# A linear recurrence in chunks: one state update for two heads, values and state in tiles of their own, and a binding on the output weights' preparation

## The chip, the cores and the metric

The kernel runs on one core of one Trainium2 chip. Its metric is the device time of one execution in microseconds (us). Three runs of the kernel before took 1298.18, 1294.85 and 1297.59 us, median 1297.59. The profile is of one further execution, which took 1294.26 us.

The engines are TensorE (PE in the profile; PEld is its loading of weights), VectorE (DVE), ScalarE (ACT) and GpSimd (POOL); SyncE (SP) issues most transfers, in the order of one queue.

## The reference, cut to what matters

One layer mixes 2048 tokens of width 1024 in three ways, gates the results and projects them. The change touches the first two ways, which are one recurrence with different sizes (GLA: 4 heads, keys of 64, values of 128; HGRN: 4 heads, keys and values of 64):

```python
CHUNK = 64
h = rms_norm(x) * (1.0 + scale[:, None, :]) + shift[:, None, :]
p = h @ w_in[l]                                  # 1024 -> 3600 columns
...
def chunk_gated_linear_attn(q, k, v, g):
    ...
    def step(state, inp):
        q_c, k_c, v_c, g_c = inp
        b_cum = jnp.cumsum(g_c, axis=2)
        decay = jnp.exp(jnp.where(causal, diff, -jnp.inf))
        scores = jnp.einsum('bhtd,bhsd,bhtsd->bhts', q_c, k_c, decay)
        o_c = (jnp.einsum('bhts,bhsv->bhtv', scores, v_c)
               + jnp.einsum('bhtd,bhdv->bhtv', q_c * jnp.exp(b_cum), state))
        b_last = b_cum[:, :, -1:, :]
        state = (jnp.exp(b_last[:, :, 0, :, None]) * state
                 + jnp.einsum('bhsd,bhsv->bhdv', k_c * jnp.exp(b_last - b_cum), v_c))
        return state, o_c
...
o_a = merge_heads(rms_norm(o_a) * gla_norm_w[l]) * jax.nn.silu(ga)
y = jnp.concatenate([o_a, o_b, o_c], axis=-1) @ w_out[l]
x = x + gate[:, None, :] * y
```

So an output of a chunk is scores times values plus decayed queries times the state, and the state goes from chunk to chunk.

## The kernel before

The work runs in stages. Projections come first: queries and keys to about 205 us, values and attention columns to about 385 us. The forget stage (to about 449 us) makes the running sums of the decays (`decay_sums`, L527 to L537): a scan gives bc; picked columns SM and their exponentials SE hold three numbers per chunk and channel. SE's middle third is the decay over a whole chunk; L533 copies it into SX, crossing it to the other 64 partitions. Then the stick-breaking attention runs to about 870 us, the recurrence from 870 to 1058 us, and the output projection to the end.

**The recurrence** (`gla_fast`, `gla_tail`) takes 16 groups, here numbered 0 to 15, of 512 tokens in 8 chunks of 64. Four groups make a pair of heads; groups 0 to 7 are GLA, 8 to 15 HGRN. The two heads of a pair lie on partitions 0 to 63 and 64 to 127. Per group:

- SP loads bc (decay sums), qt (queries), kt (keys), Vn (values, tokens on partitions) and W (L824, L825).
- ACT, DVE and POOL make eP (scaled queries, L901 or L906), eN (scaled keys, written into bc or kt) and kd (keys for the state); DVE writes M's half of decayed queries (L909).
- PE forms the scores scp (L917). ACT copies them to S, and POOL writes their causal part into M's other half.
- PE transposes kd (ptk, L836), ACT copies it to KTt, and PE multiplies it by Vn to U (L847), the increments of the state.
- DVE makes the states one chunk after another (L858): one instruction per chunk and head, on 64 partitions each.
- PE multiplies W by M (L870): one matmul of contraction depth 128 per chunk and head, scores and values on one half of the rows, queries and state on the other. The state of head h stands on the half opposite to the head, so that head's values fit on its own half.

The tiles U are single-buffered: the U of a group waits for the state updates of the group before. W has two buffers, so the load of W for a group waits for o of the group two before.

**Order.** PE's order here is written out by hand (`manual_schedule`): scp and ptk of a group, three gate steps (nine matmuls of L260), U, nine more, o of the group before, and then the next group. These gate steps are projections that fill PE; their weights come over SP into tiles tagged `wraw` and are split on ACT (whi) and DVE (wlo). On DVE, ACT, POOL and SP the order comes from a scheduler that places instructions by its own model of time.

**Output weights.** `scale_wo(0)` is started at group 8 and goes one step in each of groups 8 to 11. A step loads 512 KB of w_out into wr (L1019), which has the same tag `wraw` and so the same two buffers as the gate weights; POOL multiplies it by the gate row; DVE makes wh (L1023) and wl (L1024). The tag's turn in this stretch is: gate weights of j = 4, wr of steps 0 and 1, gate weights of j = 5, wr of steps 2 and 3, gate weights of j = 6 and 7. The gates' steps reach j = 5 at the end of the first nine matmuls of group 10, j = 6 at the start of group 13 and j = 7 in group 15. A buffer is free for its next load when DVE has made the wlo or wl of its last contents.

Of the kernel before, what the change touches and what calls it, by code (L numbers as in the profile page):

```python
# [42 lines left out]
def hybrid_mixer_kernel(ctx, tc, x, c, w_ada, b_ada, w_in, w2, bg, gnw, lbl, hnw,  # L43
# [764 lines left out]
    def load_values(pools, pr, g, GT, Wn):  # L808
# [8 lines left out]
        def new_w():  # L817
            return [pools.tile([P, NB, dv], F32, tag=f"W{h}", name=f"W{h}", bufs=2) for h in range(2)]
        W = Wn if Wn is not None else new_w()
        if Wn is None:  # L820
            nc.gpsimd.memset(W[0][64:128, 0, :], 0.0)
            nc.gpsimd.memset(W[1][0:64, 0, :], 0.0)
        vr = vcols.rearrange("(n p) d -> p n d", p=CB)
        nc.sync.dma_start(W[0][0:64], vr[:, :, 0:dv])  # L824
        nc.sync.dma_start(W[1][64:128], vr[:, :, dv:2 * dv])  # L825
        return Vn, W, new_w() if g + 1 < T // GT else None

    def gla_tail(gr_, pp, pr, g, GT, M, kd, dec, Vn, W, Wn):
# [48 lines left out]
    def gla_fast(pairs, gp, gr_, pp, scp):  # L877

        for pr in pairs:
# [3 lines left out]
            Wn = None  # L883
            for g in range(T // GTF):
# [42 lines left out]
                yield gla_tail(gr_, pp, pr, g, GTF, M, kd, SX[:, pr, g, :], Vn, W, Wn)

    def gla_exact(gp, pp):
# [5 lines left out]
        M = gp.tile([P, 2, GT + NB], F32, name="M")  # L935
        nc.gpsimd.memset(M, 0.0)
        for pr in (2, 3, 0, 1):
# [3 lines left out]
            Wn = None  # L941
            for g in range(T // GT):
# [25 lines left out]
                def level(Xk, Xq, mi):  # L968
# [6 lines left out]
                    for h in range(2):  # L975
                        hs = slice(h * 64, (h + 1) * 64)
                        nc.vector.copy_predicated(
                            v3(M[hs, h, 0:GT]), mx[hs, mi:mi + 1, :].broadcast_to((64, NB, CB)), sc[hs])
# [23 lines left out]
                for h in range(2):  # L1002
                    nc.vector.tensor_copy(M[(1 - h) * 64:(2 - h) * 64, h, :], Qs[h * 64:(h + 1) * 64, :])
                dec = gp.tile([P, NB], F32, tag="dec", name="dec")
                for h in range(2):
                    orow = slice((1 - h) * 64, (2 - h) * 64)
                    nc.vector.tensor_copy(dec[orow], M[orow, h, GT:GT + NB])
                for _ in gla_tail(gp, pp, pr, g, GT, M, kt, dec, Vn, W, Wn):
# [309 lines left out]
```

## Time and profile before

| | us |
|---|---|
| median of three runs | 1297.59 |
| the profiled execution | 1294.26 |
| its span on the core | 1292.2 |
| PE busy | 1212.9 (94%) |
| PEld busy | 991.8 (77%) |
| DVE busy | 742.1 (57%) |
| ACT busy | 471.7 (37%) |
| POOL busy | 162.9 (13%) |

The profiled execution has 2.1 us around its span. The busy shares are means over stages with different limits: a stage is read by its own windows, its chain of waits, and the timeline of the engine that waits. In the rows below a line such as "L870" is one of the kernel before; a releaser behind "<-" is what ended the idle time before the instruction.

### The profile page before, as it was taken

How to read it: one execution, taken by the hardware profiler on the slowest of the kernel's cores; microseconds unless marked ns; L12 is line 12 of the kernel's file. 1: busy time of each engine (PE TensorE's matmuls, PEld its weight loads, DVE VectorE, ACT ScalarE, POOL GpSimd, SP SyncE). 2: the span in 40 equal slices, each digit the busy share in tenths (PEclk: the TensorE clock that was granted, in tenths of full speed). 3: DMA queues.
4: the chain of work that ended last, by engine and by line, in shares of the span. 5: the costliest groups of instructions: out<-in, count | busy, mean ns of one | idle time of the engine just before them, and what ended most of it. 6: DMA issues, size and time to landing. Idle time of an engine off the chain costs nothing.

```text
span 1292.2 us, 22081 instructions
## 1 busy us (share of the span) xinstructions
PE 1212.9 (94%) x8682; PEld 991.8 (77%) x8682; DVE 742.1 (57%) x1268; ACT 471.7 (37%) x860; POOL 162.9 (13%) x197
## 2 busy tenths in 40 slices
PE   7899999999999789999999999998978897999997
PEld 7777789899998667777777776766867774777775
DVE  4866325700009873535545488877776768765652
ACT  3376423421115342322333244543333434253621
POOL 3210000000003300000000001012432312010000
PEclk8999999999999989999999999998988997999999
DMA  9765442422133341322323323127877657464621
GB/s 265 240 232 180 147 126 91 143 82 86 46 99 112 126 106 54 92 72 86 100 68 86 109 73 92 34 62 238 264 222 208 195 174 241 133 224 132 203 82 51
DMA packets 177566, 173.73 MB, mean 134 GB/s; under 512 B 39625, under 2 KB 131882, under 8 KB 177454
## 3 DMA queue, kind: packets, MB, share of 16 engines
q1 hardware_dynamic: 144970, 128.70, 33.7%
q10 hardware_dynamic: 32484, 43.54, 9.7%
q8 instruction: 70, 1.15, 0.4%
q14 instruction: 42, 0.34, 0.1%
HBM read 113.47 MB, written 58.73 MB: 133 GB/s over the span
## 4 chain that ended last, share of the span: by engine, by line
PE 62%; DVE 13%; DMA 6%; issue 5%; ACT 2%; POOL 1%; SPq 0%; ACTq 0%; POOLq 0%; DVEq 0%
PE av L750 6%; PE acc L154 5%; PE acc L156 5%; PE acc L155 5%; PE acc L166 4%; PE acc L168 4%; PE acc L167 4%; PE pt L738 4%; PE acc L260 4%; PE y L1194 4%; PE y L1192 4%; PE y L1193 4%; DMA kt<-s_kb 2%; DVE W L858 2%; DVE f L734 2%
## 5 line engine op out<-in xcount | busy, mean ns | idle before, releaser
L734 DVE TENSOR_TENSOR_SCAN f<-f 128x512 f32<-128x512 f32 (+3 forms) x160 | 169.9, 1091 | 22.0 <-ACT f L728 11.9
L154 PE MATMUL acc<-hTh,whi 128*128 128x512 f32 x400 | 160.1, 402 | 9.9 <-ACT st L185 4.3
L156 PE MATMUL acc<-hTh,wlo 128*128 128x512 f32 x400 | 157.5, 394 | 0.0
L155 PE MATMUL acc<-hTl,whi 128*128 128x512 f32 x400 | 157.4, 394 | 0.0
L166 PE MATMUL acc<-whi,hTh 128*128 128x256 f32 (+1 forms) x512 | 146.2, 285 | 1.5 <-ACT stt L193 1.5
L168 PE MATMUL acc<-whi,hTl 128*128 128x256 f32 (+1 forms) x512 | 145.8, 285 | 0.0
L167 PE MATMUL acc<-wlo,hTh 128*128 128x256 f32 (+1 forms) x512 | 145.6, 284 | 0.0
L260 PE MATMUL acc<-hTh,whi 128*128 128x512 f32 x240 | 103.8, 432 | 1.7 <-ACT hTh L244 1.7
L260 PE MATMUL acc<-hTl,whi 128*128 128x512 f32 x240 | 97.9, 408 | 4.3 <-DVE hTl L250 4.3
L1192 PE MATMUL y<-wh,hTh 128*128 128x512 f32 x256 | 101.8, 398 | 0.0
L1193 PE MATMUL y<-wl,hTh 128*128 128x512 f32 x256 | 101.6, 397 | 0.0
L728 ACT ACTIVATE f<-zt 128x512 f32<-128x512 f32 (+3 forms) x160 | 82.1, 537 | 52.9 <-DVE f L734 24.7
L1194 PE MATMUL y<-wh,hTl 128*128 128x512 f32 x256 | 100.1, 395 | 0.4 <-DVE hTl L1160 0.4
L166 PEld LDWEIGHTS acc<-whi,hTh 128*128 128x128 f32 x512 | 97.8, 191 | 1.9 <-ACT stt L193 1.7
L154 PEld LDWEIGHTS acc<-hTh,whi 128*128 128x128 f32 x400 | 75.5, 189 | 29.9 <-ACT st L185 5.6
L167 PEld LDWEIGHTS acc<-wlo,hTh 128*128 128x128 f32 x512 | 97.8, 191 | 0.1
L168 PEld LDWEIGHTS acc<-whi,hTl 128*128 128x128 f32 x512 | 97.8, 191 | 0.1
L260 PE MATMUL acc<-hTh,wlo 128*128 128x512 f32 x240 | 97.4, 406 | 0.0
L750 PE MATMUL av<-PT,V 128*64 128x128 f32 x960 | 89.7, 282 | 0.6 <-DVE PT L743 0.6
L156 PEld LDWEIGHTS acc<-hTh,wlo 128*128 128x128 f32 x400 | 75.3, 188 | 17.0 <-issue 1.4
L738 PE MATMUL pt<-ident,f 128*128 128x128 f32 x544 | 87.0, 283 | 0.9 <-DVE f L734 0.7
L155 PEld LDWEIGHTS acc<-hTl,whi 128*128 128x128 f32 x400 | 75.6, 189 | 15.2 <-issue 1.0
(206 smaller groups left out, 2106.8 us busy)
## 6 DMA issues: line engine op xcount, KB each, us to landing
wraw<-in_w_in_dram SPq DMA_DIRECT2D x36, 512.0 KB, 4.9
xt<-in_x_dram SPq DMA_DIRECT2D x16, 512.0 KB, 5.2
wa<-in_w_ada_dram SPq DMA_DIRECT2D x16, 512.0 KB, 5.6
Q<-s_qc SPq DMA_DIRECT2D x64, 128.0 KB, 3.1
ot<-s_o SPq DMA_DIRECT2D x32, 256.0 KB, 3.4
gt<-s_gate SPq DMA_DIRECT2D x32, 256.0 KB, 4.2
r<-in_x_dram SPq DMA_DIRECT2D x16, 512.0 KB, 5.6
out_dram<-r SPq DMA_DIRECT2D x15, 512.0 KB, 2.7
```

The costliest lines, as they stand in the source:

```text
L154: mm(ps, hi[:, k, :], th[:, k, :], start=(k == 0), stop=False)
L155: mm(ps, hi[:, k, :], tl[:, k, :], start=False, stop=False)
L156: mm(ps, lo[:, k, :], th[:, k, :], start=False, stop=(k == KT - 1))
L166: mm(o, th[:, k, s], hi[:, k, 0:ncols], start=(k == 0), stop=False)
L167: mm(o, th[:, k, s], lo[:, k, 0:ncols], start=False, stop=False)
L168: mm(o, tl[:, k, s], hi[:, k, 0:ncols], start=False, stop=(k == KT - 1))
L260: mm(ps, a[:, k, :], b[:, k, :], start=(k == 0 and i == 0), stop=(k == KT - 1 and i == 2))
L734: nc.vector.tensor_tensor_scan(fr, fr, fr, carry[u], op0=ALU.mult, op1=ALU.bypass)
L750: last[0] = mm(av[u * 64:(u + 1) * 64, :], (Dd if diag else V)[J][:, b, :], PT[:, b, :], start=diag, stop=(J == 0 and b == 0))
L1192: mm(y, oh[:, k, us], wh, start=(k == 0), stop=False)
L1193: mm(y, oh[:, k, us], wl, start=False, stop=False)
L1194: mm(y, ol[:, k, us], wh, start=False, stop=(k == KT - 1))
```

## The change

SX and its 32 copies are gone. W is parted into Vv (values, each head on its own half) and St (states of both heads in one tile, each on its own half). The U of a head goes to its own half, so one DVE instruction of 128 partitions updates both heads' states: 124 instead of 248 of L858. M is parted into Ms (causal scores) and Qd (decayed queries); Qd takes one instruction of 128 partitions instead of two of 64. Each matmul of o becomes two of contraction depth 64 that add up: Ms with Vv, then Qd with St. That is 32 a group instead of 16; as a float32 matmul is two passes here (L870 has 256 rows in eight groups), 64 passes instead of 32. The step of `scale_wo(0)` in groups 8 to 11 is issued under `issue_after` with the group's last state update. This binds instructions on that update's engine, DVE: wh and wl of a step stand behind the updates of its group. Loads and POOL's product are not bound. The memset of the first state is one instead of two; `rp0` and `open_h` change places. The same edits are made in the branch for strong decays (`gla_exact`), of which the trace has no row.

The core of the diff:

```diff
-        for h in range(2):
-            nc.vector.tensor_copy(SX[(1 - h) * 64:(2 - h) * 64, pr, n, :],
-                                  SE[h * 64:(h + 1) * 64, pr, n, NBF:2 * NBF])
...
-        def new_w():
-            return [pools.tile([P, NB, dv], F32, tag=f"W{h}", name=f"W{h}", bufs=2) for h in range(2)]
-        W = Wn if Wn is not None else new_w()
-        if Wn is None:
...
+
+        def new_s():
+            return pools.tile([P, NB, dv], F32, tag="St", name="St", bufs=2)
+        St = Sn
+        if St is None:
+            St = new_s()
+            nc.gpsimd.memset(St[:, 0, :], 0.0)
+        Vv = pools.tile([P, NB, dv], F32, tag="Vv", name="Vv", bufs=2)
         vr = vcols.rearrange("(n p) d -> p n d", p=CB)
-        nc.sync.dma_start(W[0][0:64], vr[:, :, 0:dv])
-        nc.sync.dma_start(W[1][64:128], vr[:, :, dv:2 * dv])
-        return Vn, W, new_w() if g + 1 < T // GT else None
-
-    def gla_tail(gr_, pp, pr, g, GT, M, kd, dec, Vn, W, Wn):
+        for h in range(2):
+            nc.sync.dma_start(Vv[h * 64:(h + 1) * 64], vr[:, :, h * dv:(h + 1) * dv])
+        return Vn, Vv, St, new_s() if g + 1 < T // GT else None
...
             for h in range(2):
-                orow = slice((1 - h) * 64, (1 - h) * 64 + 64)
-                mm(U[n % 2][orow, n // 2, :], KTt[rs, n // 2, h * 64:(h + 1) * 64],
+                mm(U[n % 2][h * 64:(h + 1) * 64, n // 2, :], KTt[rs, n // 2, h * 64:(h + 1) * 64],
                    Vn[rs, n // 2, h * dv:(h + 1) * dv], start=True, stop=True)
         for n in range(NB):
-            for h in range(2):
-                orow = slice((1 - h) * 64, (1 - h) * 64 + 64)
-                if n + 1 < NB:
-                    dst = W[h][orow, n + 1, :]
...
-                nc.vector.scalar_tensor_tensor(dst, W[h][orow, n, :], dec[orow, n:n + 1],
-                                               U[n % 2][orow, n // 2, :],
-                                               op0=ALU.mult, op1=ALU.add)
+            if n + 1 < NB:
+                dst = St[:, n + 1, :]
+            elif Sn is not None:
+                dst = Sn[:, 0, :]
+            else:
+                continue
+            om[0] = nc.vector.scalar_tensor_tensor(dst, St[:, n, :], dec[:, n:n + 1], U[n % 2][:, n // 2, :],
+                                           op0=ALU.mult, op1=ALU.add)
         yield
 
...
-        o = pp.tile([P, no, GT], F32, tag="o", name="o")
+        o = pp.tile([P, no, 512], F32, tag="o", name="o")[:, :, 0:GT]
         for n in range(NB):
             ns = slice(n * CB, (n + 1) * CB)
-            for h in range(2):
-                dst = o[:, h, ns] if gla else o[h * 64:(h + 1) * 64, 0, ns]
-                mm(dst, W[h][:, n, :], M[:, h, ns], start=True, stop=True)
+            for x, y, first in ((Vv, Ms, True), (St, Qd, False)):
+                for h in range(2):
+                    hs = slice(h * 64, (h + 1) * 64)
+                    dst = o[:, h, ns] if gla else o[hs, 0, ns]
+                    mm(dst, x[hs, n, :], y[hs, ns], start=first, stop=not first)
```
```diff
-                M = gr_.tile([P, 2, GTF], F32, tag="M", name="M", bufs=3)
+                Ms, Qd = (gr_.tile([P, GTF], F32, tag=t, name=t, bufs=3) for t in ("Ms", "Qd"))
...
-                for h in range(2):
-                    nc.vector.tensor_tensor(v3(M[(1 - h) * 64:(2 - h) * 64, h, :]),
-                                            v3(eP[h * 64:(h + 1) * 64]),
-                                            per_chunk(0)[h * 64:(h + 1) * 64], op=ALU.mult)
+                nc.vector.tensor_tensor(v3(Qd), v3(eP), per_chunk(0), op=ALU.mult)
...
-                    nc.gpsimd.affine_select(v3(M[hs, h, :]), v3(S[hs]),
+                    nc.gpsimd.affine_select(v3(Ms[hs]), v3(S[hs]),
                                             pattern=[[0, NBF], [1, CB]], base=0,
                                             channel_multiplier=-1, compare_op=ALU.is_ge, fill=0.0)
-                yield gla_tail(gr_, pp, pr, g, GTF, M, kd, SX[:, pr, g, :], Vn, W, Wn)
+                yield gla_tail(gr_, pp, pr, g, GTF, Ms, Qd, kd, SE[:, pr, g, NBF:2 * NBF],
+                               Vn, Vv, St, Sn)
...
                     ws = scale_wo(0, pw0, gr_.tile([P, 512], F32, name="gb", bufs=1))
-                next(ws, None)
+                if i >= 8:
+                    with tc.issue_after(om[0].ins):
+                        next(ws, None)
```

The scheduler's order changes with it. On DVE, in group 5, the order before mixes updates of both heads with other work; W_8966 and W_8967 are the two heads' tiles, U_9178 and U_9179 even and odd chunks, wh_9948 and wl_9949 output weights, eP and bc of group 7.

```order
L858 SCALAR_TENSOR_TENSOR W_8966<-W_8966,SX,U_9178 64x128
L901 SCALAR_TENSOR_TENSOR eP<-qt,eP 128x512
L858 SCALAR_TENSOR_TENSOR W_8967<-W_8967,SX,U_9178 64x128
L1023 CAST wh_9948<-wr 128x1024
L858 SCALAR_TENSOR_TENSOR W_8966<-W_8966,SX,U_9179 64x128
L902 TENSOR_TENSOR bc<-kt,bc 128x512
L858 SCALAR_TENSOR_TENSOR W_8967<-W_8967,SX,U_9179 64x128
L1024 TENSOR_TENSOR wl_9949<-wr,wh_9948 128x1024
L858 SCALAR_TENSOR_TENSOR W_8966<-W_8966,SX,U_9178 64x128
L858 SCALAR_TENSOR_TENSOR W_8967<-W_8967,SX,U_9178 64x128
L858 SCALAR_TENSOR_TENSOR W_8966<-W_8966,SX,U_9179 64x128
L909 TENSOR_TENSOR M<-eP,SE 64x512 x2
```

After the change the same work stands on DVE like this in HGRN's groups 8 and 9 (St<-St,SE,U with U_9621 and U_9622 are updates of group 8, with U_9780 and U_9781 of group 9; wlo is the split of gate weights j = 5; Qd belongs to group 10, eP to group 11):

```order
L855 SCALAR_TENSOR_TENSOR St<-St,SE,U_9622 128x64
L855 SCALAR_TENSOR_TENSOR St<-St,SE,U_9621 128x64
L855 SCALAR_TENSOR_TENSOR St<-St,SE,U_9622 128x64
L855 SCALAR_TENSOR_TENSOR St<-St,SE,U_9621 128x64
L855 SCALAR_TENSOR_TENSOR St<-St,SE,U_9622 128x64
L1011 CAST wh_9652<-wr 128x1024
L906 TENSOR_TENSOR Qd<-eP,SE 128x512
L1012 TENSOR_TENSOR wl_9653<-wr,wh_9652 128x1024
L141 TENSOR_TENSOR wlo<-wraw,whi 128x1024
L904 TENSOR_TENSOR eP<-qt,eP 128x512
L855 SCALAR_TENSOR_TENSOR St<-St,SE,U_9780 128x64
L855 SCALAR_TENSOR_TENSOR St<-St,SE,U_9781 128x64
```

The updates now stand together, wh and wl have moved from the GLA groups to right behind the updates of groups 8 to 11, and wlo of j = 5 stands between wl of step 0 and the next eP.

On SP, in GLA's groups 4 to 7, the queue before has the wraw of j = 5 ahead of bc of group 6, and the wr of step 2 ahead of bc of group 7 (bc_75 and kt_67 are the second GLA pair's, qt_70 an HGRN pair's):

```order
L824 DMA W_8960<-s_va 64x8x128
L825 DMA W_8961<-s_va 64x8x128
L140 DMA wraw<-in_w_in_dram 128x8x128
L887 DMA bc<-s_da_75 128x512
L889 DMA kt<-s_ka_67 128x512
L815 DMA Vn<-s_va 128x4x256
L888 DMA qt<-s_qb_70 128x512
L824 DMA W_8966<-s_va 64x8x128
L825 DMA W_8967<-s_va 64x8x128
L1019 DMA wr<-in_w_out_dram 128x2x512
L887 DMA bc<-s_da_75 128x512
L889 DMA kt<-s_ka_67 128x512
```

The queue after has no wraw there, and the wr of step 1 in the place of that of step 2:

```order
L823 DMA Vv<-s_va 64x8x128 x2
L885 DMA bc<-s_da_75 128x512
L887 DMA kt<-s_ka_67 128x512
L886 DMA qt<-s_qb_70 128x512
L811 DMA Vn<-s_va 128x4x256
L1007 DMA wr<-in_w_out_dram 128x2x512
L823 DMA Vv<-s_va 64x8x128 x2
L885 DMA bc<-s_da_75 128x512
L887 DMA kt<-s_ka_67 128x512
L886 DMA qt<-s_qb_70 128x512
```

The wraw of j = 5 has left this stretch, and bc of group 6 follows Vv of group 4 directly.

On SP in HGRN's groups, the queue before holds only the group's own loads from W of group 9 (W_9546) to bc of group 12 (kt_78 are the first HGRN pair's keys, kt_79 the second's, whose first group is 12):

```order
L824 DMA W_9546<-s_ib 64x8x64
L825 DMA W_9547<-s_ib 64x8x64
L889 DMA kt<-s_kb_78 128x512
L887 DMA bc<-s_db_76 128x512
L815 DMA Vn<-s_ib 128x4x128
L888 DMA qt<-s_qb_71 128x512
L824 DMA W_9693<-s_ib 64x8x64
L825 DMA W_9694<-s_ib 64x8x64
L889 DMA kt<-s_kb_79 128x512
L887 DMA bc<-s_db_77 128x512
```

The queue after, from Vv of group 9 to wr of step 3:

```order
L823 DMA Vv<-s_ib 64x8x64 x2
L139 DMA wraw<-in_w_in_dram 128x8x128
L887 DMA kt<-s_kb_78 128x512
L885 DMA bc<-s_db_76 128x512
L1007 DMA wr<-in_w_out_dram 128x2x512
L811 DMA Vn<-s_ib 128x4x128
L886 DMA qt<-s_qb_71 128x512
L823 DMA Vv<-s_ib 64x8x64 x2
L887 DMA kt<-s_kb_79 128x512
L885 DMA bc<-s_db_77 128x512
L1007 DMA wr<-in_w_out_dram 128x2x512
```

The wraw of j = 5 and the wr of steps 2 and 3 now stand ahead of the keys and decay sums of groups 11, 12 and 13; the wraw of j = 6 and j = 7 follow ahead of those of group 14.

## Rows read from the trace of the kernel before

**Rows 1.** Windows: start:end, length, PE, PEld, DVE, ACT, POOL busy, clock, DMA, GB/s.
```profile
389.00:448.50 59.50, 51.90 (x219) 41.40 (x218) 54.86 (x90) 25.93 (x45) 22.54 (x15) 0.97 0.33 115
878.10:980.50 102.40, 88.23 (x1169) 74.30 (x1168) 78.51 (x163) 32.48 (x56) 34.37 (x32) 0.92 0.81 237
980.50:1058.10 77.60, 69.74 (x1234) 55.94 (x1233) 55.60 (x164) 27.57 (x47) 21.24 (x27) 0.96 0.67 194
```

**Rows 2.** Groups by line and shape from 840 to 1070 us.
```profile
L858 DVE SCALAR_TENSOR_TENSOR W<-W,SX,U 64x128 f32<-64x128 f32 x124 | 43.0, 347 | 7.7 <-PE U L847 3.4 <-PE o L870 0.5
L858 DVE SCALAR_TENSOR_TENSOR W<-W,SX,U 64x64 f32<-64x64 f32 x124 | 34.7, 280 | 7.4 <-PE U L847 3.4
L870 PEld LDWEIGHTS o<-M,W 128*128 128x128 f32 x256 | 29.9, 192 | 0.7
...
L909 DVE TENSOR_TENSOR M<-eP,SE 64x512 f32<-64x512 f32 x32 | 26.4, 826 | 0.8
...
L870 PEld LDWEIGHTS o<-M,W 128*64 128x64 f32 x256 | 8.3, 139 | 3.6 <-issue 2.8 <-POOL rh L1150 0.9
...
L1024 DVE TENSOR_TENSOR wl<-wr,wh 128x1024 fp32r<-128x1024 f32 x4 | 5.2, 1302 | 0.1
...
L1023 DVE CAST wh<-wr 128x1024 fp32r<-128x1024 f32 x4 | 3.3, 817 | 3.8 <-POOL wr L1020 3.8
```

**Rows 3.** Timeline of PE, 889 to 980 us, columns are start, length, instruction.
```profile
890.47 0.44 PE L847 MATMUL U<-Vn,KTt 64*64 64x128 f32 x4 [1.64 <-ACT KTt L838]
894.15 1.97 PE L847 MATMUL U<-Vn,KTt 64*64 64x128 f32 x28 [3.24 <-DVE W L858]
...
902.85 1.09 PE L917 MATMUL scp<-eP,bc 64*32 64x64 f32 x64
...
906.52 1.10 PE L847 MATMUL U<-Vn,KTt 64*64 64x128 f32 x32
...
913.36 1.09 PE L917 MATMUL scp<-eP,bc 64*32 64x64 f32 x64
...
935.20 1.09 PE L917 MATMUL scp<-eP,bc 64*32 64x64 f32 x64
...
945.34 2.68 PE L847 MATMUL U<-Vn,KTt 64*64 64x128 f32 x32 [6.40 <-issue]
...
954.43 1.09 PE L917 MATMUL scp<-eP,bc 64*32 64x64 f32 x64
...
966.09 1.09 PE L917 MATMUL scp<-eP,bc 64*32 64x64 f32 x64
```

**Rows 4.** Timeline of SP's queue in the same stretch.
```profile
925.25 0.63 SPq L825 DMA_DIRECT2D W<-s_va  x1
931.11 0.39 SPq L140 DMA_DIRECT2D wraw<-in_w_in_dram  x1
```

**Rows 5.** Chain of waits, the GLA and HGRN stretches, columns are start, length, work.
```profile
899.40 3.52 PE o L870 x32
...
1047.39 1.08 PE o L870 x32
...
1052.16 0.62 PE U L847 x32
...
1055.05 1.13 PE o L870 x32
```

**Rows 6.** Timeline of all engines, 994.7 to 1006 us.
```profile
994.77 0.65 SPq L889 DMA_DIRECT2D kt<-s_kb  x1
...
1002.72 0.69 DVE L906 TENSOR_TENSOR eP<-qt,eP 128x512 f32<-128x512 f32 x1 [3.04 <-ACT eP L897]
```

**Rows 7.** DMA issues on the page, columns are count, KB, us to landing.
```profile
wraw<-in_w_in_dram SPq DMA_DIRECT2D x36, 512.0 KB, 4.9
```

**Rows 8.** The forget stage's copies by line, and SP's waits behind it.
```profile
L533 DVE COPY SX<-SE 64x8 f32<-64x8 f32 x16 | 5.8, 364 | 0.4
...
SPq L696 <- DMA s_db<-bc: 17.5, 1, 17.5
```

More of the change, by code (lines that the diff above doesn't have):

```diff
@@ L94, in hybrid_mixer_kernel @@
     SE = const.tile([P, 4, T // GTF, 3 * NBF], F32, name="SE")
-    SX = const.tile([P, 4, T // GTF, NBF], F32, name="SX")
     ada_b = const.tile([P, 16], F32, name="ada_b")
@@ L108, in hybrid_mixer_kernel @@
     hpools = [None] * NCH
-    rp0 = ctx.enter_context(tc.tile_pool(name="rp0", bufs=1, side="right"))
-    rp0.tile([P, 8], F32, name="shift")
     def open_h(n):
@@ L118, in open_h @@
                  hp.tile([P, KT, 512], F32R, name=f"hTl{n}"))
+    rp0 = ctx.enter_context(tc.tile_pool(name="rp0", bufs=1, side="right"))
+    rp0.tile([P, 8], F32, name="shift")
     open_h(ORDER[0])
@@ L805, in hybrid_mixer_kernel, with load_values @@
     hpools[ORDER[2]].close()
-    def load_values(pools, pr, g, GT, Wn):
+    def load_values(pools, pr, g, GT, Sn):
         gla = pr < 2
@@ L815, in load_values, with gla_tail @@
         nc.sync.dma_start(Vn, vcols.rearrange("(b p) d -> p b d", p=P))
[L817 to L828 removed]
+        def new_s():
[5 more added lines that the diff above has]
+        Vv = pools.tile([P, NB, dv], F32, tag="Vv", name="Vv", bufs=2)
+        vr = vcols.rearrange("(n p) d -> p n d", p=CB)
+        for h in range(2):
+            nc.sync.dma_start(Vv[h * 64:(h + 1) * 64], vr[:, :, h * dv:(h + 1) * dv])
+        return Vn, Vv, St, new_s() if g + 1 < T // GT else None
+    om = [None]
+    def gla_tail(gr_, pp, pr, g, GT, Ms, Qd, kd, dec, Vn, Vv, St, Sn):
         gla = pr < 2
@@ L882, in gla_fast @@
             s = 1.0 / 16.0 if gla else 1.0
-            Wn = None
+            Sn = None
             for g in range(T // GTF):
@@ L889, in gla_fast @@
                 nc.sync.dma_start(kt, s_feat["ka" if gla else "kb"][j][:, tsl])
-                Vn, W, Wn = load_values(gr_, pr, g, GTF, Wn)
+                Vn, Vv, St, Sn = load_values(gr_, pr, g, GTF, Sn)
                 def per_chunk(i):
                     return SE[:, pr, g, i * NBF:(i + 1) * NBF].unsqueeze(2).broadcast_to((P, NBF, CB))
-                M = gr_.tile([P, 2, GTF], F32, tag="M", name="M", bufs=3)
+                Ms, Qd = (gr_.tile([P, GTF], F32, tag=t, name=t, bufs=3) for t in ("Ms", "Qd"))
                 eP = gp.tile([P, GTF], F32, tag="eP", name="eP")
@@ L934, in gla_exact @@
         nc.sync.dma_start(mx, masks)
-        M = gp.tile([P, 2, GT + NB], F32, name="M")
-        nc.gpsimd.memset(M, 0.0)
+        Ms = gp.tile([P, GT], F32, name="Ms")
+        nc.gpsimd.memset(Ms, 0.0)
         for pr in (2, 3, 0, 1):
@@ L940, in gla_exact @@
             s = 1.0 / 16.0 if gla else 1.0
-            Wn = None
+            Sn = None
             for g in range(T // GT):
@@ L950, in gla_exact @@
                 nc.sync.dma_start(qt, s_feat["qa" if gla else "qb"][j][:, tsl])
-                Vn, W, Wn = load_values(gp, pr, g, GT, Wn)
+                Vn, Vv, St, Sn = load_values(gp, pr, g, GT, Sn)
                 if gla:
@@ L974, in level @@
                             mm(sc[hs, n, :], Xk[hs, ns], Xq[hs, ns], start=True, stop=True)
[L975 to L978, printed above, removed]
+                    nc.vector.copy_predicated(
+                        v3(Ms), mx[:, mi:mi + 1, :].broadcast_to((P, NB, CB)), sc)
                 for lv in range(6):
@@ L1001, in gla_exact @@
                 nc.vector.tensor_tensor(kt, kt, dd, op=ALU.mult)
[L1002 to L1008, printed above, removed]
+                for _ in gla_tail(gp, pp, pr, g, GT, Ms, Qs, kt, Qs[:, GT:GT + NB], Vn, Vv, St, Sn):
                     pass
```

4 lines of the change are left out of this document (removed).

## Prediction

> **What bounds the kernel now.** I read the windows of the stages first, then the groups by line inside the recurrence, then the timelines of PE, SP and all engines around its long waits, and last its chain of waits. Two stretches hold nearly all that the change touches: GLA's groups, 102.40 us with PE busy 88.23 and DVE 78.51, and HGRN's, 77.60 with 69.74 and 55.60 [rows 1]. PE is the bound in both, but GLA's groups are far from even. A clean one takes 10.51 us from scp to scp (902.85 to 913.36). Group 1 reaches its U at 890.47, does four passes, then stands 3.24 us behind the updates of the group before. Group 5 takes 19.23 us (935.20 to 954.43): PE is idle 6.40 us ahead of U, and U's 32 passes take 2.68 us instead of 1.10. Group 7, from 966.09 to the stretch's end at 980.5, takes 14.4 [rows 1, 3]. SP tells why group 5 is late: W is issued until 925.88, the next transfer, gate weights, starts at 931.11 [rows 4], and the decay sums of group 6 stand right behind it in the queue. DVE's order puts eP of later groups between the updates, so late decay sums hold the updates, and these hold the next U. HGRN's clean period is 7.66 us, o to o, 1047.39 to 1055.05 [rows 5].
>
> **GLA's groups, gains.** The updates' 124 instructions of 347 ns and 124 of 280 become 62 of each [rows 2]; I take the same duration for 128 partitions as for 64, since each partition has as many elements as before (bounds: the same, or twice it, by which DVE would save nothing). That is 8 x 0.347 = 2.8 us a group less on DVE, and Qd saves 0.83 [rows 2]. PE sees this only where U waits for it.
> - Group 1: U starts at 890.47 and a clean group needs 6.84 us from U to the next scp (906.52 to 913.36), so scp could come at 897.3 instead of 902.85 [rows 3]: -5.5.
> - Group 5: no gate weights stand ahead of the decay sums of group 6, so 19.23 falls to a clean 10.6: -8.6.
> - Group 7: 14.4 to 10.6: -3.8.
> - New: the wr of step 1 stands ahead of bc of group 7 and waits for a wlo: I take +1.0; its bounds are 0 and the 5.2 us that gate weights stood in that place (925.88 to 931.11) [rows 4].
>
> **o on PE.** 32 passes in GLA take 3.52 us, 110 ns each, with weight loads of 128 columns (192 ns each); in HGRN 1.08 us, with 64 columns (139 ns) [rows 2, 5]. Now there are 64 passes of 64 rows. Whether two on different row halves run at once is not shown for o, but it is for U, whose tiles are 64 by 64: 32 passes in 0.62 us, 19 ns each [rows 5]. Tiles on two column halves alone leave 34 ns a pass (HGRN's o before, 1.08 / 32) [rows 5], so in U the row halves overlap too. I take GLA's o as 32 x 110 ns + 0.2 = 3.7, +0.1 to 0.2 in each of eight groups, +1.0 in all. HGRN's o before already ran two tiles at once; now its two diagonal quarters do, half the columns at a time: 32 x 55 ns + 0.2 = 2.0, +0.9 x 8 = +7.2. The bounds are the 3.52 and 1.08 of before, since no column of output goes, and 7.0 and some 3.5 us, where row halves do not overlap.
> The weight loads are where the pages speak against the change: the Trainium skill (TensorE: Matmul & The Clock Gate, LDWEIGHTS) says that a load's time goes by columns and not by contraction depth, so that half the rows save nothing. The trace agrees on columns (192 ns for 128, 139 for 64 [rows 2]) and has no row on depth; by that rule alone o doubles, which is the rival D below. The Trainium skill (TensorEngine Tiling (Array Packing), Tiling Modes, Key Properties) also lets different tiles load and multiply in parallel. U's 0.62 us [rows 5] agrees, and by it o stays near the values taken.
>
> GLA's sum: -5.5 - 8.6 - 3.8 + 1.0 + 1.0, and -1.2 for short waits of U behind updates in the other groups, = -17.1. The stretch would take 85.3, still over the 8 x 10.51 = 84.1 of clean groups.
>
> **HGRN's groups, losses.** A clean period becomes 7.66 + 0.9 = 8.5. Here four loads that stood in GLA's groups come ahead of the groups' own, each waiting for a wl or wlo of DVE, which itself now stands behind updates.
> - U(11). Count from the end of eP(11) on DVE. The updates of group 9 take 8 x 0.30 = 2.4 (280 ns and a short gap), wh 0.82, Qd 0.83, wl 1.30 [rows 2]: 5.3. Then wr of step 2 may start, Vn, qt and two Vv follow it in SP's queue (five issues of about 0.5, [rows 4, 6]), so kt(12) is issued at 7.9. From the issue of such a kt to the end of the next eP took 8.6 us (994.77 to 1003.41) [rows 6]; I use 7.5 to 8.6, so eP(12) ends at 15.4 to 16.5. Six updates of group 10 stand behind it (1.8): U(11) at about 17.2 or later. PE without a wait: U(10) at 2.4, and a period of 8.5 later, 10.9. Stall 6.3.
> - U(10): the updates of group 9 stand behind wlo of j = 5, whose load waits for wl of step 0. From the start of the updates of group 8: 5.3 to the end of wl, 0.4 + 4.9 to the landing [rows 7], whi and wlo 0.8 each (by wh's row, of the same shape), eP 0.7, updates 2.4: 15.3 against 16.4 for PE's two periods less U. By this count it just fits; as it hangs on a load and on three engines' turns I take 2.5, between 0 and the 6.3 of U(11).
> - U(12): the last update of group 11 stands behind wlo of j = 6, whose load waits for wl of step 2. From U(11): 2.95 (wh, Qd, wl) + 0.4 + 4.9 + 0.8 + 0.8 + 0.3 = 10.2 against 8.5 [rows 2, 7]: 1.9 with the queue.
> - U(13): the same with wraw of j = 7, and bc(14) behind that load, two Vv and a wr; S and KTt of group 13 on ACT stand behind whi and eP of group 14. From U(12): bc(14) issued at some 4.5, eP(14) by 12.1 with the 7.5 above, three updates and wlo 1.7, S and KTt 1.3 (an estimate, two copies behind eP): 15.1 against 8.5: 6.6.
> Together 17.3. While PE stands still its clock falls in this kernel (U's 2.68 instead of 1.10 us behind 6.40 idle [rows 3]); two such waits, 1.5. Eight clean periods are 61.3; 3 us more are my estimate for the last group's tail and what stays of short waits, so the floor without the change is 64.3 (61.3 to 77.6). 64.3 + 7.2 + 17.3 + 1.5 = 90.3, +12.7. Bounds: if the four waits cost nothing, 71.5 (-6.1); if each costs 7, 101 (+23.4).
>
> **The forget stage.** 32 copies go, 16 of them here: 5.8 us of a DVE busy 54.86 of 59.50 us [rows 1, 8]. PE is busy 51.90, so not all returns; the range is 0 to -5.8, and I take the middle, -3.0, because the row is nearer to a full engine than to an idle one. What follows starts later only by one transfer chain: SP waits 17.5 us for the last store of decay sums [rows 8], and that store moves with DVE. The other 16 copies lie in the values stage beside PE's matmuls: 0. The output projection starts from the last stores of the recurrence and moves with them: 0.
>
> **Sum.** -17.1 + 12.7 - 3.0 = -7.4. The profiled execution of 1294.26 us, span 1292.2, would be 1286.9; the median of the runs stands 3.3 above it, so 1297.6 - 7.4 = 1290.2.
>
> **Rivals.**
> - B, the four waits in HGRN cost next to nothing, because DVE with half its updates runs ahead and transfers are issued early enough. For it: DVE is busy 55.60 of 77.60 [rows 1] and loses 62 x 0.28 = 17.4. Against it: the waits are set by the binding and the queue's order, not by DVE's load. -17.1 - 6.1 - 3.0 gives -26; with a third of the waits left, -20: 1277.
> - C, no change: each of the four waits takes as long as U(13)'s, 6.5 us, since one late load delays every later one in SP's queue. 64.3 + 7.2 + 26 + 1.5 = 99.0, +21.4; -17.1 + 21.4 - 3.0 = +1.3: 1299. For it: in group 5 one such load cost 8.6 us. Against it: PE's periods are longer by 0.9, which gives each load more time.
> - D, slower: the loads of 128 columns on the two row halves do not overlap. GLA's o takes 7.0 instead of 3.7, +26, HGRN's 3.5 instead of 2.0, +12. PE's longer periods then cover waits in HGRN: some -12 of the 17.3. -7.4 + 26 + 12 - 12 = +19: 1316. It decides from an o of GLA of about 4.6 us on, where 0.9 x 8 eats the gain. For it: a single load takes 192 ns [rows 2]. Against it: before, loads already followed each other every 110 ns [rows 5].
>
> **How the numbers follow.** The forecast has 0.45 (its own range 1284 to 1296), B 0.20, C 0.20, D 0.15. A measurement of this kernel can tell about 0.3%, 3.9 us, from no change. Faster by more holds B, most of the forecast (0.37) and little of C (0.02): 0.59; slower holds D and some of C (0.06): 0.21; the same 0.20. The range reaches into B and C and the lower half of D: 1274 to 1309.
>
> **What would show it.** Right: U of group 5 without idle time ahead of it; o of GLA near 3.7 us and of HGRN near 2.0; waits of SP ahead of wr and wraw in HGRN's groups, with PE idle ahead of U of groups 11 and 13; GLA's stretch near 85 us, HGRN's near 90. Wrong: an o of GLA above 4.6 us, updates of 128 partitions that take longer than 347 or 280 ns, or HGRN's stretch under 75.

## The result, and the profile after

The changed kernel took 1308.99 us (median of 6 runs, 1304.60 to 1313.07) against 1297.60 for the kernel before (6 runs): a ratio of 1.0089, 95% interval 1.0062 to 1.0116. It is slower by 11.4 us, where 1290.2 and so 7.4 us faster had been forecast; the median stands at the upper edge of the range (1309).

The profiled execution took 1313.07 us (span 1311.2), 4.1 above its median, where that of before stood 3.3 below its own. So the stages below differ by 19.0 us in sum, 7.6 more than the medians. scp(0) is the time of the first scp of group 0; GLA goes from there to scp of group 8, HGRN to the end of the last o, y is the first matmul of the output projection. The names e1 to e13 are the experiments below.

| profiled execution | scp(0) at | GLA | HGRN | o to y | y to end | span |
|---|---|---|---|---|---|---|
| before | 878.1 | 102.4 | 77.6 | 25.2 | 208.8 | 1292.2 |
| after | 872.2 | 106.5 | 94.2 | 28.5 | 209.8 | 1311.2 |
| difference | -5.9 | +4.0 | +16.6 | +3.2 | +1.0 | +19.0 |
| forecast | -3.0 | -17.1 | +12.7 | 0 | 0 | -7.4 |
| e2, before with the binding | 875.9 | 97.7 | 80.6 | 26.6 | 209.7 | 1290.5 |
| e1, after without the binding | 870.8 | 121.0 | 84.4 | 29.4 | 209.6 | 1315.1 |
| e13, after with Vn ahead of qt | 871.8 | 96.5 | 90.2 | 28.0 | 209.1 | 1295.5 |
| e5, after with qt behind kt | 871.2 | 92.2 | 83.8 | 27.8 | 210.0 | 1285.0 |

The windows of the same three stretches after (columns as in [rows 1]):

```profile
389.00:448.50 59.50, 55.24 (x240) 44.21 (x238) 51.45 (x75) 28.20 (x49) 24.58 (x15) 1.00 0.37 128
872.20:978.70 106.50, 90.58 (x1397) 74.96 (x1397) 39.51 (x81) 29.33 (x53) 25.31 (x27) 0.90 0.79 202
978.70:1072.90 94.20, 78.73 (x1523) 63.88 (x1521) 43.58 (x106) 30.20 (x51) 29.51 (x28) 0.95 0.67 190
```

DVE is busy 39.51 us in GLA where it was 78.51 [rows 1]: half of its work is gone from there, and the stretch is longer. The time from one scp to the next, group by group in GLA, says where (the last column ends with scp of group 8):

| scp to scp, us | 0 | 1 | 2 | 3 | 4 | 5 | 6 | 7 |
|---|---|---|---|---|---|---|---|---|
| before | 7.0 | 17.8 | 10.5 | 11.3 | 10.5 | 19.2 | 11.7 | 14.4 |
| after | 7.0 | 11.9 | 10.7 | 16.9 | 16.6 | 12.7 | 18.8 | 11.9 |
| e2 | 7.0 | 18.4 | 10.5 | 12.1 | 10.5 | 17.2 | 11.1 | 10.9 |
| e13 | 7.0 | 14.4 | 10.7 | 12.9 | 17.2 | 10.9 | 12.2 | 11.0 |
| e5 | 7.0 | 13.5 | 10.7 | 12.3 | 14.7 | 10.7 | 12.6 | 10.7 |

Groups 1, 5 and 7, which had been long, are shorter; groups 3, 4 and 6, which had been clean or nearly so, are long. There PE stands ahead of U, while U of group 5, behind 6.40 us of idle time before [rows 3], now comes after 1.20 and 0.32 (U of groups 3, 4, 5 and 6):

```profile
909.03 2.38 PE L846 MATMUL U<-Vn,KTt 64*64 64x128 f32 x32 [3.47 <-issue]
...
925.59 1.98 PE L846 MATMUL U<-Vn,KTt 64*64 64x128 f32 x32 [3.17 <-ACT KTt L838]
...
940.23 0.44 PE L846 MATMUL U<-Vn,KTt 64*64 64x128 f32 x4 [1.20 <-ACT KTt L838]
...
957.44 2.37 PE L846 MATMUL U<-Vn,KTt 64*64 64x128 f32 x32 [5.71 <-ACT KTt L838]
```

The groups that answer to [rows 2]:

```profile
L855 DVE SCALAR_TENSOR_TENSOR St<-St,SE,U 128x128 f32<-128x128 f32 x62 | 21.5, 347 | 2.6
...
L868 PEld LDWEIGHTS o<-Ms,Vv 64*128 64x128 f32 x256 | 19.6, 188 | 3.1 <-issue 2.7 <-DMA s_gate<-st 0.4
L855 DVE SCALAR_TENSOR_TENSOR St<-St,SE,U 128x64 f32<-128x64 f32 x62 | 17.3, 280 | 10.6 <-PE U L846 6.1 <-PE o L868 2.0
...
L906 DVE TENSOR_TENSOR Qd<-eP,SE 128x512 f32<-128x512 f32 x16 | 14.1, 884 | 0.0
...
L868 PEld LDWEIGHTS o<-Ms,Vv 64*64 64x64 f32 x256 | 13.2, 135 | 3.7 <-issue 2.8 <-POOL rh L1140 0.8
```

An update of 128 partitions takes exactly what one of 64 took, 347 and 280 ns, and there are half as many. The chain of waits has GLA's o of group 1, HGRN's last o, and two loads:

```profile
887.44 3.72 PE o L868 x64
...
909.18 11.31 DMA bc<-s_da
...
924.32 10.44 DMA bc<-s_da
...
1050.73 2.09 PE o L868 x64
```

An o of GLA has 64 passes in 3.72 us (3.52 with 32 passes before [rows 5]), one of HGRN in 2.09. What is new on the chain is the weight of the loads of bc: they are 61% of it in GLA's stretch, 10 to 11 us each for groups 5 to 7, where they were 17% before, 5 to 7 us each. The waits of PE and, in GLA, of SP's queue (in all, times, longest):

```profile
PE U L846 <- ACT KTt L838: 22.9, 10, 5.7
PE U L846 <- issue: 3.5, 1, 3.5
```

```profile
SPq L886 <- DVE eP L899: 37.5, 5, 10.3
...
SPq L1007 <- DVE St L855: 6.8, 2, 3.9
```

In group 1 U waited for the updates of the group before [rows 3]; now U waits for KTt, and SP for eP (L886 is the load of qt). KTt of a group stands on ACT behind the exponentials of bc of the next group, in both kernels: when that bc is late, ACT stands, then KTt, then U. Here are SP's queue in one turn, and DVE and ACT beside it:

```profile
921.96 0.32 SPq L886 DMA_DIRECT2D qt<-s_qa  x1
922.37 0.39 SPq L811 DMA_DIRECT2D Vn<-s_va  x1
922.85 1.34 SPq L823 DMA_DIRECT2D Vv<-s_va  x2
924.32 1.72 SPq L885 DMA_DIRECT2D bc<-s_da  x1
926.56 0.33 SPq L887 DMA_DIRECT2D kt<-s_ka  x1
```

```profile
921.24 0.69 DVE L899 SCALAR_TENSOR_TENSOR eP<-qt,eP 128x512 f32<-128x512 f32 x1 [11.25 <-ACT eP L895]
```

```profile
920.57 0.63 ACT L895 ACTIVATE eP<-bc 128x512 f32<-128x512 f32 x1 [13.38 <-DMA bc<-s_da]
...
924.95 0.59 ACT L838 COPY KTt<-ptk 128x512 f32<-128x512 f32 x1
```

eP of group 5 ends at 921.93 after a wait of 11.25 us. At 921.96 SP lets qt of group 7 go, which had stood at the queue's head for this eP, and right behind it Vn (512 KB), two Vv (512 KB) and bc of group 6. That bc lands after 10.44 us, and the next eP, which waits for it, ends at 936.2. This is a ring: eP, a qt that waits for it, what stands behind qt in SP's queue, the load of bc, the next eP. Its turns in groups 4 to 8 took 18.7, 14.3, 17.8 and 14.0 us (ends of eP at 903.2, 921.9, 936.2, 954.0 and 968.0), where PE needs 10.7. The two long turns also hold a wr (L1007, steps 0 and 1), at which SP stood 2.9 and 3.9 us until DVE had made a wlo (done at 906.31 and 940.68, the wr let go at 906.33 and 940.71; the row names the update that starts beside it).

### The profile page after: what moved, and what is told of

Read it like the earlier page. It is cut to its first block, busy times and chain, and to the rows that moved or that the text cites. A ratio compares the mean times of both kernels' runs of the same rounds, so it can differ in the third digit from the quotient of the medians.

```text
span 1311.2 us, 22887 instructions
## 1 busy us (share of the span) xinstructions
PE 1224.5 (93%) x9194; PEld 998.8 (76%) x9194; DVE 677.6 (52%) x1096; ACT 471.1 (36%) x860; POOL 162.1 (12%) x193
## 4 chain that ended last, share of the span: by engine, by line
PE 61%; DMA 14%; DVE 11%; issue 6%; ACT 4%; SPq 2%; POOL 1%; ACTq 0%; POOLq 0%; DVEq 0%
PE av L746 5%; PE acc L153 5%; PE acc L155 5%; PE acc L154 5%; PE acc L165 5%; PE acc L167 5%; PE acc L166 5%; PE pt L734 4%; PE y L1182 4%; PE y L1183 4%; PE y L1184 4%; PE acc L259 4%; DMA bc<-s_da 4%; DMA bc<-s_db 2%; DVE f L730 2%
## 5 line engine op out<-in xcount | busy, mean ns | idle before, releaser
L730 DVE TENSOR_TENSOR_SCAN f<-f 128x512 f32<-128x512 f32 (+3 forms) x160 | 169.9, 1091 | 22.1 <-ACT f L724 12.3
L734 PE MATMUL pt<-ident,f 128*128 128x128 f32 x544 | 86.9, 283 | 0.9 <-DVE f L730 0.7
```

Source lines behind the costliest of these rows:

```text
L730: nc.vector.tensor_tensor_scan(fr, fr, fr, carry[u], op0=ALU.mult, op1=ALU.bypass)
```

## The experiments

**e1: the binding taken away.**

```diff
-                if i >= 8:
-                    with tc.issue_after(om[0].ins):
-                        next(ws, None)
+                next(ws, None)
```

> The changed kernel with the output weights' steps unbound again (from group 4 on the scheduler places wh and wl of a step where it likes, as before the change). Theory 1 (the binding puts the waits of SP for wl into HGRN's groups): HGRN from scp of group 8 to the last o falls from 94 to about 80 us, GLA from scp of group 0 to scp of group 8 stays near 104 to 108, in all about 1298. Rival (HGRN is slow for its 64-row matmuls of o and not for the binding): HGRN stays at 90 or more, about 1309.

1317.97 us, ratio 1.0177 (1.0145 to 1.0209): slower still. HGRN fell to 84.4 as theory 1 has it, but GLA rose to 121.0. In group 5 (DVE, then PE):

```profile
954.02 1.12 DVE L1011 CAST wh<-wr 128x1024 fp32r<-128x1024 f32 x1 [9.44 <-POOL wr L1008]
...
956.65 0.34 DVE L855 SCALAR_TENSOR_TENSOR St<-St,SE,U 128x128 f32<-128x128 f32 x1
```

```profile
957.04 1.97 PE L846 MATMUL U<-Vn,KTt 64*64 64x128 f32 x28 [12.22 <-DVE St L855]
```

The last update of group 4 (956.65) stands on DVE behind a wh whose wr had not come, and U of group 5 waited 12.22 us for it. The binding is no loss by itself: it keeps such a wh away from GLA's updates (GLA 106.5 for 121.0), and costs less than that in HGRN (94.2 for 84.4).

**e2: the binding alone, in the kernel before.**

```diff
-                nc.vector.scalar_tensor_tensor(dst, W[h][orow, n, :], ...)
+                om[0] = nc.vector.scalar_tensor_tensor(dst, W[h][orow, n, :], ...)
...
-                next(ws, None)
+                if i >= 8:
+                    with tc.issue_after(om[0].ins):
+                        next(ws, None)
```

> The kernel before with the binding alone (wh and wl of a step behind the last state update of groups 8 to 11; everything else as it was). Theory 1: HGRN rises from 77.6 to 88 or more, GLA falls a little from 102 (two loads less in its queue) to 95 to 102; in all 1300 to 1306. Rival: HGRN stays near 78, so the binding is harmless by itself; about 1293.

1292.85 us, ratio 0.9972 (0.9958 to 0.9986): faster. GLA gains 4.7, HGRN loses 3.0. So with the binding in both kernels, the new tiles cost 16.1 us by the medians (1308.99 against 1292.85); of the 20.7 us between the profiled spans, 8.7 are in GLA and 13.6 in HGRN.

**e3: three buffers for qt.**

```diff
+ gp.tile([P, GTF], F32, tag=t, name=t, bufs=3 if t == "qt" else 2)
```

> The changed kernel with three buffers for qt instead of two, so that a load of qt in SP's queue waits for eP of a group one earlier. Theory 2 (in GLA the load of bc stands behind a qt that waits for eP of the group before, so that the groups run one after another through a load of 8 to 11 us): GLA falls from 106 to 88 to 94, in all about 1295. Rival (the loads are slow because the transfers' bandwidth is used up, whatever their order): GLA stays within 3 us of 106, in all about 1308.

1307.30 us, ratio 1.0080 (1.0052 to 1.0107), GLA 107.0. It told nothing on theory 2: with the third buffer the scheduler placed each qt a group earlier in SP's queue, so that it waited for the same eP ahead of the same bc.

**e4: buffers of their own for the output weights' loads.**

```diff
-            wr = wp.tile([P, 2, 512], F32, tag="wraw", name="wr")
+            wr = gr_.tile([P, 2, 512], F32, tag="wr", name="wr")     # in this stretch only
```

> The changed kernel with the output weights' loads of this stretch in two buffers of their own, not in those of the gate weights; the binding stays. Theory 1 in its narrow form (it is the turn of the two shared buffers, wraw waiting for wl and wr for wlo, that makes SP stand): HGRN falls from 94 to 80 to 85, GLA stays near 104, in all about 1298. Rival (the binding itself, since wh and wl stand between the updates on DVE): HGRN stays over 90.

1304.75 us, ratio 1.0059 (1.0038 to 1.0080). HGRN fell from 94.2 to 88.6, less than theory 1 wanted; GLA took 104.6.

**e5: qt behind kt.**

```diff
-                nc.sync.dma_start(qt, ...)
-                nc.sync.dma_start(kt, ...)
+                with tc.issue_after(kl[0].ins) if kl[0] is not None else ExitStack():
+                    nc.sync.dma_start(qt, ...)
+                kl[0] = nc.sync.dma_start(kt, ...)
```

> The changed kernel with each load of qt bound behind the loads of bc and kt of the group before in SP's queue (from group 4 on the queue reads bc, kt, then qt of the next group, where it read qt, then Vn, two Vv and bc). The experiment with three buffers left that order as it was, because the scheduler moved each qt one group ahead. Theory 2 (bc waits in SP's queue behind a qt that waits for eP of the group before, a ring of eP, SP's queue, the load of bc, and the next eP): GLA falls from 106 to 88 to 95, HGRN from 94 by a few us; in all 1293 to 1299. Rival 2 (the ring is not what holds GLA; the loads are slow by their sum of bytes): GLA stays above 103.

1286.55 us, ratio 0.9913 (0.9879 to 0.9947): faster than both kernels, and by more than expected. GLA took 92.2, HGRN 83.8.

```profile
871.30:963.50 92.20, 84.64 (x1396) 70.42 (x1397) 41.02 (x86) 31.49 (x55) 25.42 (x28) 0.98 0.82 237
963.50:1047.30 83.80, 76.04 (x1523) 62.22 (x1521) 44.23 (x102) 28.67 (x48) 28.35 (x27) 0.96 0.71 211
```

```profile
915.24 2.16 SPq L823 DMA_DIRECT2D Vv<-s_va  x2
917.51 0.56 SPq L887 DMA_DIRECT2D bc<-s_da  x1
918.21 0.34 SPq L890 DMA_DIRECT2D kt<-s_ka  x1
920.64 0.32 SPq L889 DMA_DIRECT2D qt<-s_qa  x1
```

bc of group 6 (917.51) is let go ahead of the qt of group 7, which waits for eP of group 5 in the changed kernel, and is there 5.8 us later. The ring is cut by one group's lead; theory 2 stands. A good part of HGRN's loss went with it. (On DVE the scheduler moved two eP and a wlo by up to three places.)

**e6: Vn left out for three groups of four.**

```diff
+        if Sn is None:
+            vk[0] = pools.tile(...); nc.sync.dma_start(vk[0], ...)
+        Vn = vk[0]
```

> The changed kernel with Vn (values with tokens on partitions, 512 KB in GLA) loaded for the first group of each pair only and used for all four; the state's increments of the other groups are made from those values. SP's queue holds the same waits, but 512 KB less right ahead of each bc. Theory 2a (bc is slow because Vn was let go together with it behind qt): a bc of groups 4 to 8 lands after 5 to 7 us instead of 8.5 to 11.4, GLA falls from 106 to about 90 to 95, in all 1290 to 1298. Rival 2b (bc's length of load is only a small part, the wait for qt is all): GLA stays above 102.

1295.62 us, ratio 0.9992 (0.9977 to 1.0008). GLA took 95.5, as 2a has it, but bc of groups 4 to 8 still landed after 8.8, 8.3, 9.5, 8.3 and 7.1 us, for 8.6, 11.4, 10.5, 10.1 and 9.9 in the changed kernel. The time speaks for 2a, the loads only in part, as none but the last came near the 5 to 7 expected: inconclusive.

**e7 and e8: qt behind kt with e4's buffers, and in the kernel before with the binding.** The edits are e5's and e4's, and e5's and e2's.

> Both cures together in the changed kernel: own buffers for the output weights' loads and qt behind kt; the binding stays. If the two waits are separate: GLA 88 to 95, HGRN 80 to 87, in all 1283 to 1291, below the kernel before. If both only move the wait: 1300 or more.

1289.00 us, ratio 0.9932 (0.9913 to 0.9950): GLA 94.7, HGRN 86.9. The two cures don't add up; own buffers give nothing beside e5.

> The kernel before (one tile of values and state per head, two updates a chunk) with the binding and with qt behind kt. Theory 2: GLA falls from 97.7 by a few us only, since its bc landed after 6 to 8 us already, in all 1288 to 1293. Rival: the older structure gains as much from it as the new one, 10 us or more.

1291.02 us, ratio 0.9949 (0.9928 to 0.9969); GLA 97.5 against 97.7 in e2. In the older tiles GLA as a whole gained nothing by cutting the ring.

**e9: SX's copies put back into the changed kernel** (a single run).

```diff
+        for h in range(2):
+            nc.vector.tensor_copy(SX[(1 - h) * 64:(2 - h) * 64, pr, n, :], SE[...])
```

> The changed kernel with the 32 copies from SE to SX put back (nothing reads SX). If the copies' removal is what makes the recurrence start earlier: scp of group 0 moves from 872 back to 876 to 878. If the earlier start is from another edit or from chance: it stays at 870 to 873. The recurrence itself should stay as in the changed kernel (GLA over 102, HGRN over 90).

scp(0) came at 877.5, as expected; in the changed kernel and the six others with the new tiles and no SX run up to then it came at 869.9 to 872.2, and in the three others with SX (before, e2, e8) at 875.9 to 878.1. The copies were worth about 6 us. GLA took 104.6 and HGRN 97.4, in all 1315.4.

**e10: qt behind kt, the weights' steps in groups 12 to 15.** On top of e5:

```diff
-                if i >= 8:
+                if i >= 12:
```

> qt behind kt, and the output weights' four steps in groups 12 to 15 in place of 8 to 11, still bound. Theory 1 (the loads wr and wraw that wait for wl and wlo are what is left of HGRN's loss besides the longer o): HGRN falls from 83.8 with qt behind kt alone to 75 to 79, GLA stays at 90 to 95, o to y stays under 30; in all 1280 to 1285. Rival (o and the longer chain of HGRN's own loads hold it): HGRN stays at 82 or more, in all 1286.

1291.36 us, ratio 0.9953 (0.9935 to 0.9972). Groups 10 to 13 now run without a wait, 8.6 us each; rows of PE, one group apart:

```profile
986.21 1.09 PE L915 MATMUL scp<-eP,kt 64*32 64x64 f32 x64
...
994.80 1.09 PE L915 MATMUL scp<-eP,kt 64*32 64x64 f32 x64
...
1003.37 1.09 PE L915 MATMUL scp<-eP,kt 64*32 64x64 f32 x64
...
1011.94 1.09 PE L915 MATMUL scp<-eP,kt 64*32 64x64 f32 x64
...
1020.52 1.09 PE L915 MATMUL scp<-eP,kt 64*32 64x64 f32 x64
```

But groups 14 and 15 pay it back: U of group 14 waits 3.11 us, and the gate weights of j = 7 are let go at 1038.48, when the wl of the third step is done (1038.41), so that PE stands 4.01 us behind their whi. HGRN took 89.0. Theory 1 is right on who waits, the rival on the sum.

**e11: qt behind kt and three buffers for qt.** e5's and e3's edits.

> qt behind kt, and three buffers for qt, so that a qt waits for eP of three groups before and hardly ever stops SP's queue. Theory 2 (the ring through qt is the bound of GLA): with it cut altogether GLA falls below the 92.2 of qt behind kt alone, to 84 to 90, in all 1279 to 1285. Rival (at one group's lead the ring is slack already, and loads of 6 to 9 us behind o and its buffers hold the rest): GLA 91 to 94, in all 1286.

1286.76 us, ratio 0.9931 (0.9911 to 0.9951), GLA 92.5: the rival's numbers. With a lead of one group the ring is slack.

**e12: qt behind kt, own buffers, no binding.** The edits of e5, e4 and e1.

> qt behind kt, own buffers for the output weights' loads, and no binding: all four loads go out ahead of group 4, wh and wl stand between the updates of groups 1 to 3. If the binding only kept wh and wl away from GLA's updates: groups 1 to 4 of GLA lose 8 to 15 us against qt behind kt alone, HGRN falls to 75 to 80; in all 1285 to 1293. Rival (with its own buffers the preparation is hidden beside PE wherever it stands): GLA 90 to 93 and HGRN under 80, in all 1278 to 1283.

1291.83 us, ratio 0.9952 (0.9934 to 0.9971). GLA took 103.8, HGRN 80.4: the first expectation, HGRN at its edge. In group 2, U's last 28 passes wait for an update that stands behind wh and wl:

```profile
898.30 0.43 PE L846 MATMUL U<-Vn,KTt 64*64 64x128 f32 x4
907.42 1.97 PE L846 MATMUL U<-Vn,KTt 64*64 64x128 f32 x28 [8.69 <-DVE St L855]
```

**e13: Vn ahead of qt again.** The orders of PE, DVE, ACT and POOL stay as after the change.

```diff
+                with tc.issue_after(vl[-2].ins) if len(vl) > 1 else ExitStack():     # vl: the loads of Vn
+                    nc.sync.dma_start(qt, ...)
```

> The changed kernel with each qt bound behind the load of Vn of two groups before: in GLA SP's queue reads Vn, qt, Vv, bc, as the kernel before had it in most groups, where the changed kernel reads qt, Vn, Vv, bc. The waits of qt, and the orders of DVE and ACT, stay as in the changed kernel. Theory 3 (the ring through qt was there before too, at about 11 us a turn; what the change did is to put Vn's 512 KB between the waiting qt and bc, so that a turn takes 14 to 18): GLA falls from 106 to 94 to 99, in all 1297 to 1302, most of what qt behind kt gave in GLA. Rival 3 (Vn's place is nothing; the shorter run of updates and DVE's new order make the ring long): GLA stays above 103, in all 1306 or more.

1294.51 us, ratio 0.9972 (0.9955 to 0.9990): 14.5 us under the changed kernel's median. GLA took 96.5, as theory 3 has it. In the turn that took 14.3 us after the change:

```profile
915.18 0.37 SPq L813 DMA_DIRECT2D Vn<-s_va  x1
920.96 0.32 SPq L889 DMA_DIRECT2D qt<-s_qa  x1
921.37 1.34 SPq L825 DMA_DIRECT2D Vv<-s_va  x2
922.82 0.65 SPq L887 DMA_DIRECT2D bc<-s_da  x1
```

Vn goes at 915.18, while SP waits; behind qt stand only Vv and bc, which lands after 7.0 us instead of 10.4; the turn takes 10.2. The two turns without a wr fell from 14.3 and 14.0 to 10.2 and 11.1, the two with one only from 18.7 and 17.8 to 17.3 and 15.2.

## Why the prediction was wrong

**The step that failed is GLA's sum of -17.1: the groups that it did not name were held at a clean 10.6 us, and the rest of SP's queue was priced as it had been.** The named gains came in the main: group 1 -5.9 for -5.5, group 5 -6.5 for -8.6, group 7 -2.6 for -3.8. But groups 3, 4 and 6, in which the sum had only -1.2 for short waits and +1.0 for the wr of step 1, took 5.6, 6.1 and 7.2 us more. Measured: GLA +4.0 where -17.1 stood.

The edits of the tiles let the scheduler move two things past each other: before, SP's queue read Vn, qt, W, bc in most turns; after, qt, Vn, Vv, bc. The two pieces of SP's order in the section on the change show it. I read in them only that a wraw was gone. With Vn between a qt that waits and the bc behind it, a turn of the ring took 14.0 and 14.3 us, and 17.8 and 18.7 with a wr in it as well. e13 turns back this one thing and has GLA at 96.5, 10.0 less; in all it takes 14.5 us less, of the 18.8 between forecast and result, and is 3.6 us faster than the kernel before, about half of the 7.4 forecast. e5 cuts the ring, and has 92.2.

**The wr's in GLA were the smaller part of the same step.** For the wr of step 1 +1.0 stood in the sum, for that of step 0 nothing; SP stood 3.9 and 2.9 us at them, with the next bc behind it in the queue. Vn's place doesn't explain this part: group 4, whose U waits behind the turn with the wr of step 0, still takes 17.2 us in e13 and 14.7 in e5, where SP stands 10.9 and 9.1 us at that wr. No experiment takes the weights' loads out of this place alone.

**What the moved wr and wraw gave.** By e2, GLA's gain from the binding alone is 4.7 us: group 5 went from 19.2 to 17.2 us only, without a wraw in its queue, and group 7 from 14.4 to 10.9. In the new tiles the binding gives GLA more, 14.6 (121.0 to 106.5); there the unbound order sets an update behind a wh (e1).

**HGRN's losses were near in sum, +16.6 for +12.7, in part by luck: the four waits came to 9.8 us for 17.3, and lay elsewhere.** PE's idle time ahead of U was 2.08, 0.84, 4.66 and 2.25 us in groups 10 to 13, where 2.5, 6.3, 1.9 and 6.6 had been forecast. The rows of PE, and DVE's waits for the loads named (wlo of j = 5, and eP of groups 12 and 14):

```profile
1008.86 1.02 PE L846 MATMUL U<-Vn,KTt 64*64 64x64 f32 x32 [2.08 <-ACT st L184]
...
1020.26 1.02 PE L846 MATMUL U<-Vn,KTt 64*64 64x64 f32 x32 [0.84 <-ACT KTt L838]
...
1033.92 1.13 PE L846 MATMUL U<-Vn,KTt 64*64 64x64 f32 x32 [4.66 <-ACT KTt L838]
...
1046.31 0.69 PE L846 MATMUL U<-Vn,KTt 64*64 64x64 f32 x32 [2.25 <-ACT KTt L838]
```

```profile
1004.76 1.23 DVE L141 TENSOR_TENSOR wlo<-wraw,whi 128x1024 fp32r<-128x1024 f32 x1 [6.13 <-ACT whi L140]
...
1018.01 0.69 DVE L904 TENSOR_TENSOR eP<-qt,eP 128x512 f32<-128x512 f32 x1 [5.95 <-ACT eP L895]
...
1042.04 0.69 DVE L904 TENSOR_TENSOR eP<-qt,eP 128x512 f32<-128x512 f32 x1 [3.96 <-DMA kt<-s_kb]
```

Groups 8 and 9 waited 1.30 and 1.74 us ahead of U as well. Eight clean periods of 8.6 (e10; 8.5 forecast) and these six waits make 81.7 of the 94.2 us; the other 12.5, slow passes behind the waits and the tail among them, were not parted further. Part of the loss is the queue's order, not the binding: e5 and e13, both bound, have 83.8 and 90.2, and in e13 nothing but that order differs.

**o was right:** 3.72 us for 3.7 in GLA, and 2.09 for 2.0 in HGRN. The two row halves overlap: loads of 188 ns each follow one another every 58 ns, where loads of all rows followed every 110, and rival D is out. The rule of the Trainium skill on load times (TensorE: Matmul & The Clock Gate, LDWEIGHTS) holds for one load, which takes 188 ns with 64 rows where it took 192 with 128, but loads of the two halves overlap, so 64 passes took 0.2 us more than 32, not twice the time.

**SX was right in kind and too small:** 3.0 forecast (0 to 5.8), 5.9 in the trace, about 6 by e9. At the end of the forget stage the lead over before is 3.1 us in the trace (last bc at 444.8 for 447.9); by the attention's matmuls at 470.2 (475.8 before) it is 5.6, and it stays near that to the recurrence. That is nearly the whole 5.8 us of the copies, where half had been taken.

**Rivals.** None of them had this. B and C spoke of HGRN only; D was on the right side for a reason that the trace denies. The slower case that came true, Vn moved behind a waiting qt and ahead of bc, was not among them. That the time still falls inside the range, at its upper end, is luck: that end was drawn from the lower half of D.

**Left open:** what the two wr's in GLA cost by themselves, the 3.2 us more from the last o to y, which the kernels with the new tiles share in part (26.8 to 31.2 against 25.2 to 26.6), and why bc still took 7.1 to 9.5 us in e6 with Vn out of its way.

## What to carry to other kernels

Where a scheduler lays out a queue, compare the whole order of a turn before and after, not the instructions that the change names: what stands between an entry that waits and the load that the next turn needs is the price. Look for the ring (an engine's result, a load that waits for it, the loads behind that one in the queue, the same result of the next group) and work out one turn against the bound engine's period. Here binding one load behind another made the same change 22.4 us faster (1308.99 to 1286.55), a version that beats both kernels.
